# Turning merged branches, x2 and the MLP's inner layer: TensorE transposes replaced by 32x32 VectorE transposes and a pass through memory

## The chip, the cores and the metric

The kernel runs on one core of a Trainium2 chip. A core has a matrix engine (TensorE, "PE" in the profile, with its weight loads as "PEld"), a vector engine (VectorE, "DVE"), a scalar engine (ScalarE, "ACT"), GpSimd ("POOL") and SyncE ("SP"). Each runs its own instruction stream in order, and they wait for one another through semaphores. SP issues the DMAs of the weights, POOL most of the others; 16 DMA engines carry them out. SBUF is the on-chip memory of 128 partitions; PSUM holds what TensorE writes. The metric is the device time of one execution in microseconds, lower is better.

## What is computed

One layer of a decoder on 256 tokens of 2048 features, in float32. Three mixers read one input projection; their outputs are projected, gated, summed and projected again, and an MLP follows. Cut to what matters here:

```python
for l in range(DEPTH):                                   # DEPTH = 1
    u = rms_norm(x, attn_norm[l])
    proj = jnp.einsum('bsd,de->bse', u, w_in[l])
    ...
    o_fox = fox_mixer(...); o_mla = mla_mixer(...); o_gdn = gdn_mixer(...)      # each (1, 256, 1024)
    gates = jax.nn.sigmoid(gate.astype(jnp.float32)).reshape(B, S, N_BRANCHES, D_MODEL)
    merged = (gates[:, :, 0] * jnp.einsum('bsc,cd->bsd', o_fox, w_branch[l, 0])
              + gates[:, :, 1] * jnp.einsum('bsc,cd->bsd', o_mla, w_branch[l, 1])
              + gates[:, :, 2] * jnp.einsum('bsc,cd->bsd', o_gdn, w_branch[l, 2]))
    x = x + jnp.einsum('bsd,de->bse', merged, w_out[l])
    h = rms_norm(x, mlp_norm[l])
    h = jnp.square(jax.nn.relu(jnp.einsum('bsd,df->bsf', h, w_up[l])))          # (1, 256, 8192)
    x = x + jnp.einsum('bsf,fd->bsd', h, w_down[l])
return rms_norm(x, final_norm)
```

## The kernel before

**Products.** All large products run through `gemm` (L211). Weights stream from memory; the activations lie in SBUF, turned: features on the partitions, tokens along the free axis, because TensorE contracts over partitions. Activations and weights are both split into two exact parts, a high one (rounded to the type `F32R`) and the rest; three passes (high x high, high x low, low x high) are summed in PSUM. So each product needs its left side as `H` and `L`, tiles of [128 features, 16 feature tiles, 256 tokens] made by `hl_pair` (L155).

`gemm` takes a block of 512 output columns at a time, with two PSUM tiles (one for each half of the tokens, `t` = 0 and 1). A block has `KT / 2` steps (KT = 16 row tiles, 8 in the branches). In a step a weight chunk of 256 rows (`raw`, 4 buffers) is loaded by SP, ScalarE casts it to `wh` (L220), VectorE subtracts to get `wl` (L221; 3 buffers each), and TensorE runs 12 matmuls (L227 to L229). At the block's end the function `evac` is called for `t` = 0 and `t` = 1 and takes the result out of PSUM.

**Stages around the change.**
- Branches (L1002 to L1017): 4 column blocks `n`, each with 3 products `b` of KT = 8. `evac` multiplies with the sigmoid of the gates, which POOL loads from memory (L1007), and sums in `acc[t]`. After `b` = 2, `to_hl` (L990) turns `acc[t]` into the left side `mH`, `mL` of `w_out`.
- Output projection (L1026 to L1035): `out_evac` adds the product to the residual `x2` and sums squares (L1030); at `t` = 1, `transpose_pair` (L142, called at L1033) turns the 512 new columns of `x2`, multiplies with the gain of the norm and writes `hH`, `hL`.
- MLP (L1044 to L1062): 4 times, 4 blocks of `w_up`, whose `up_evac` takes relu, squares, and turns with `to_hl` into `dH`, `dL`; then 4 blocks (3 in the last round) of `w_down`.

So 512 columns that a block has produced become four row tiles of the next product. Those of the last block of a stage are needed in steps 6 and 7 of the next stage's first block.

`to_hl` does for one `t`: four TensorE transposes of 128x128 into a PSUM tile (L994), a ScalarE cast into `H` (L998) and a VectorE subtraction into `L` (L999). `transpose_pair` does the same for two column tiles and both `t`, with the gain (L147, L151, L152).

**Order.** The kernel is traced in the order of the Python code. When it is built (`schedule_with_timeline_sim=True`, L1122), a scheduler gives each engine a fixed order from a modelled timeline: among the instructions that the model holds ready, the one traced first. On the chip each engine then runs its order, whatever arrives late. Large tiles share 13 buffers of 8 KB per partition (tag "m8", made by `big`, L87); small work tiles of [128, 512] share 8 (tag "t2"). A tile whose tag has no free buffer waits until one is released.

Of the kernel before, what the change touches and what calls it, by code (L numbers as in the profile page):

```python
# [18 lines left out]
P = 128  # L19
# [14 lines left out]
WARM = 12  # L34

# [23 lines left out]
def decoder_kernel(ctx: ExitStack, tc: tile.TileContext, x, attn_norm, w_in, fox_fgate_bias, mla_q_norm,  # L59
# [73 lines left out]
    sel = cp.tile([P, 264], F32R, tag="sel", name="sel")  # 8 x [128, 32], column j of the j-th is 1  # L133
# [8 lines left out]
    def transpose_pair(src, ct0, kt0, g0, H, L):  # L142
        """Columns ct0, ct0 + 1 of src (128 each), both token tiles, times the gains g0, g0 + 1, into H/L(kt0), (kt0 + 1)."""
        pv = psx("tr").rearrange("p (a b) -> p a b", a=2)
        for a in range(2):
            for t in range(2):
                PE.transpose(pv[:, a, t * P:(t + 1) * P], src(t, ct0 + a), ident)  # L147
        for a in range(2):
            g = gcol[:, g0 + a:g0 + a + 1]
            hh = H(kt0 + a)  # L150
            A.activation(out=hh, in_=pv[:, a, :], func=AF.Copy, scale=g)  # L151
# [11 lines left out]
    def rsqrt_(dst, src, n, s):  # L163
        """dst = src ** -0.5 for [128, n] tiles of positive numbers."""
# [32 lines left out]
    def rstd_of(ss, parts, n, s, r=None):  # L197
        """(sum over the parts / n + eps) ** -0.5 per token tile -> [128, 2]."""
# [10 lines left out]
    CK = 2  # L209

    def gemm(lhsH, lhsL, W, row0, KT, blocks, evac):  # L211
        for bi, (c0, n) in enumerate(blocks):
            ps = [pm.tile([P, 512], F32, tag="mm", name=nm("mm")) for _ in range(2)]
            for kc in range(0, KT, CK):
# [7 lines left out]
                for kk in range(CK):  # L222
                    k = kc + kk
                    for t in range(2):
                        sl = slice(t * P, (t + 1) * P)
                        last = k == KT - 1
                        PE.matmul(ps[t][:, :n], lhsT=lhsH(k)[:, sl], rhs=wh[:, kk, :n], start=(k == 0), stop=False)  # L227
                        PE.matmul(ps[t][:, :n], lhsT=lhsH(k)[:, sl], rhs=wl[:, kk, :n], start=False, stop=False)  # L228
                        PE.matmul(ps[t][:, :n], lhsT=lhsL(k)[:, sl], rhs=wh[:, kk, :n], start=False, stop=last)  # L229
# [6 lines left out]
    def run(*gens):  # L236
        """Trace generators to their ends, one after another."""
# [4 lines left out]
    def weave(main, side):  # L242
        """Trace main with one step of side behind each of its steps."""
# [12 lines left out]
    def w_cols(blocks, evac):  # L256
        return gemm(uH, uL, w_in, 0, 16, blocks, evac)
# [44 lines left out]
    def softplus_parts(z, n, s):  # L302
        """log1p(exp(-|z|)) and exp(-|z|)."""
# [75 lines left out]
    lat = big("lat", tag="m8a").rearrange("p (t c) -> p t c", t=2)  # L379
    latk = sp.tile([P, 2, 72], F32, tag="latk", name="latk")  # forget logits, rotary key  # L380
# [30 lines left out]
    def load_split(src, n):  # L411
        """A weight of 512 rows, n columns at most 512, as [128, 4, n], in two exact parts: 2 x two row tiles."""
# [21 lines left out]
    def by_feature(w, H, L, dst, scale):  # L434
        """dst: [128, 4, 256] <- four heads of 128 features."""
# [22 lines left out]
    def rope(dst, src, t, nh):  # L458
        """dst, src: [128, nh, 64]."""
# [106 lines left out]
    def fox_decay():  # L566
# [5 lines left out]
        nl = small([P, 16], "nl")  # -log f  # L572
# [6 lines left out]
        ncum = small([P, 16], "ncum")  # -cumulative log f  # L579
# [14 lines left out]
    def fox():  # L594
# [72 lines left out]
    def gdn():  # L667
        V.tensor_tensor(out=zg.rearrange("p t (h d) -> p (t h) d", d=HD), in0=zg.rearrange("p t (h d) -> p (t h) d", d=HD),
                        in1=onorm.unsqueeze(1).broadcast_to([P, 16, HD]), op=ALU.mult)
        # z[:, 0] = a + dt_bias, z[:, 1] = b  # L670
# [20 lines left out]
        # cumulative log decay in each chunk of 128, and its total  # L691
# [23 lines left out]
        ex = small([P, 16], "ex")  # exp(g_total - g) of chunk 0, exp(g) of chunk 1  # L715
# [4 lines left out]
        # squared norms of k and q: columns (w, t, h)  # L720
# [32 lines left out]
        # Gram matrices  # L753
# [15 lines left out]
        # inverses of the 32 x 32 diagonal blocks by forward substitution, one block's half per partition  # L769
# [36 lines left out]
        # join them to 64 and to 128  # L806
        # (I + X')^-1 = D - D O D with O = X' between the blocks; of 128 columns, 64 change at a level
# [20 lines left out]
        def part(ap, lv, b):  # L828
            """Columns of [128, n, 128] in the even (b = 0) or odd blocks of 32 (lv = 0) or of 64 (lv = 1)."""
# [27 lines left out]
        # k of chunk 0 by tokens  # L857
# [7 lines left out]
        # outputs, chunk by chunk  # L865
# [3 lines left out]
        og = R  # a chunk's outputs take the place of its right-hand sides  # L869
# [45 lines left out]
        # scale, norm, gate  # L915
# [74 lines left out]
    def to_hl(src, H, L, n, t):  # L990
        """512 columns of a token tile, transposed, into H/L (lists of two [128, 8, 256])."""
        pt = psx("hl").rearrange("p (a t) -> p a t", a=4)
        for a in range(4):
            PE.transpose(pt[:, a, :], src[:, a * P:(a + 1) * P], ident)  # L994
        r = slice((n % 2) * 4, (n % 2) * 4 + 4)
        c = slice(t * P, (t + 1) * P)
        h = H[n // 2][:, r, c]
        A.copy(out=h, in_=pt)  # L998
        V.tensor_tensor(out=L[n // 2][:, r, c], in0=pt, in1=h.bitcast(F32), op=ALU.subtract)  # L999

    mH, mL, mHt, mLt = hl_pair("m")
    for n in range(4):  # L1002
        acc = [t2("acc") for _ in range(2)]
        for b in range(3):
            def evac(bi, t, ps, b=b, n=n, acc=acc):
# [8 lines left out]
                if b == 2:  # L1014
                    to_hl(acc[t], mHt, mLt, n, t)

            run(gemm(lambda k, b=b: oH[b][:, k, :], lambda k, b=b: oL[b][:, k, :], w_branch[0, b], 0, 8, [(n * 512, 512)], evac))  # L1017

# [7 lines left out]
    def out_evac(n, t, ps):  # L1026
# [8 lines left out]
    run(gemm(mH, mL, w_out[0], 0, 16, [(n * 512, 512) for n in range(4)], out_evac))  # L1035
# [8 lines left out]
    for c in range(4):  # L1044
        dH, dL, dHt, dLt = hl_pair("d")

        def up_evac(n, t, ps):
            r = t2("r")
            A.activation(out=r, in_=ps, func=AF.Relu)
            V.tensor_tensor(out=r, in0=r, in1=r, op=ALU.mult)  # L1050
            to_hl(r, dHt, dLt, n, t)

        run(gemm(hH, hL, w_up[0], 0, 16, [(c * 2048 + n * 512, 512) for n in range(4)], up_evac))
# [8 lines left out]
        run(gemm(dH, dL, w_down[0], c * 2048, 16, [(n * 512, 512) for n in range(4 if c < 3 else 3)], down_evac))  # L1062

# [62 lines left out]
```

## Time and profile before

| | us |
|---|---|
| timed runs, median of 3 (lowest, highest) | 1723.16 (1722.75, 1724.45) |
| span of the profiled execution, first to last instruction | 1721.6 |
| difference: median less span | 1.6 |

The page gives no time of its own for the profiled execution beside its span; what lies outside the span is put at the difference above. The granted TensorE clock is 0.997 of full speed over the span. The transposes in question show as groups of instructions:

```profile
L994 PE MATMUL hl<-cst,r x128: 270/272/273, 1027.9 to 1629.6; 128*128 128x128 f32 x128
L994 PE MATMUL hl<-cst,acc x32: 270/272/273, 814.7 to 916.1; 128*128 128x128 f32 x32
L147 PE MATMUL tr<-cst,xx x32: 270/273/273, 936.8 to 1005.8; 128*128 128x128 f32 x32
```

How to read it: a row of the answer for one tile has the line, the engine, the operation, what it writes and reads, how often, its shortest, median and longest duration in ns, and the first and last start in us. Matmuls are pipelined, and their ends are modelled, so durations of neighbours overlap; what one costs is seen in the distance between things that repeat. The chain of work that ended last follows the run backwards from its last instruction, at each step to what released it or to the instruction before it on its engine; only what lies on this chain can shorten the run directly. In a timeline row the bracket at the end gives the engine's idle time just before the instruction and what ended it.

### The profile page before, as it was taken

How to read it: one execution, taken by the hardware profiler on the slowest of the kernel's cores; microseconds unless marked ns; L12 is line 12 of the kernel's file. 1: busy time of each engine (PE TensorE's matmuls, PEld its weight loads, DVE VectorE, ACT ScalarE, POOL GpSimd, SP SyncE). 2: the span in 40 equal slices, each digit the busy share in tenths (PEclk: the TensorE clock that was granted, in tenths of full speed). 3: DMA queues.
4: the chain of work that ended last, by engine and by line, in shares of the span. 5: the costliest groups of instructions: out<-in, count | busy, mean ns of one | idle time of the engine just before them, and what ended most of it. 6: DMA issues, size and time to landing. Idle time of an engine off the chain costs nothing.

```text
span 1721.6 us, 21456 instructions
## 1 busy us (share of the span) xinstructions
PE 1705.6 (99%) x8131; PEld 1433.8 (83%) x8131; DVE 1018.7 (59%) x1388; ACT 799.7 (46%) x1019; POOL 51.6 (3%) x91
## 2 busy tenths in 40 slices
PE   8999999999999999999999999999999999999997
PEld 8997889978788898888888888888888888888886
DVE  5755455676668946646665565555555555555555
ACT  5554446555534434544544544434443344334443
POOL 1000000000010100001100000000000000000000
PEclk9999999999999999999999999999999999999999
DMA  7755464766667745767776566556655665566553
GB/s 214 211 163 181 142 177 133 223 202 179 174 177 217 220 122 158 257 218 262 243 276 201 183 184 192 186 193 190 189 186 194 190 188 186 192 193 187 185 193 140
DMA packets 183209, 331.49 MB, mean 193 GB/s; under 512 B 15577, under 2 KB 42401, under 8 KB 181953
## 3 DMA queue, kind: packets, MB, share of 16 engines
q1 hardware_dynamic: 176816, 307.54, 58.4%
q0 software_dynamic: 5968, 22.05, 3.8%
q8 instruction: 64, 1.05, 0.3%
q10 hardware_dynamic: 320, 0.53, 0.1%
q14 instruction: 41, 0.33, 0.1%
HBM read 319.05 MB, written 11.03 MB: 192 GB/s over the span
## 4 chain that ended last, share of the span: by engine, by line
PE 76%; DVE 1%; DMA 1%; issue 1%; ACT 0%; DVEq 0%; SPq 0%; ACTq 0%; POOLq 0%
PE mm L228 24%; PE mm L229 24%; PE mm L227 24%; PE hl L994 1%; DMA of<-of_d 0%; PE mm L1088 0%; PE mm L1087 0%; PE mm L1086 0%; PE pO L843 0%; PE pD L851 0%; DMA E<-gcd 0%; PE pg L762 0%; PE cv L633 0%; DVE wl L221 0%; PE oo L909 0%
## 5 line engine op out<-in xcount | busy, mean ns | idle before, releaser
L221 DVE TENSOR_TENSOR wl<-raw,wh 128x1024 fp32r<-128x1024 f32 (+4 forms) x568 | 678.8, 1196 | 557.3 <-ACT wh L220 552.2
L220 ACT CAST wh<-raw 128x1024 fp32r<-128x1024 f32 (+4 forms) x568 | 585.4, 1031 | 721.3 <-PE mm L229 680.1
L228 PE MATMUL mm<-wl,uH 128*128 128x512 f32 (+4 forms) x960 | 367.1, 383 | 1.7 <-DVE wl L221 1.6
L229 PE MATMUL mm<-wh,uL 128*128 128x512 f32 (+4 forms) x960 | 363.2, 379 | 0.0
L227 PE MATMUL mm<-wh,uH 128*128 128x512 f32 (+4 forms) x960 | 336.9, 382 | 0.0
L228 PEld LDWEIGHTS mm<-wl,uH 128*128 128x128 f32 x960 | 180.9, 188 | 32.9 <-DVE wl L221 3.1
L229 PEld LDWEIGHTS mm<-wh,uL 128*128 128x128 f32 x960 | 180.9, 189 | 29.5
L227 PEld LDWEIGHTS mm<-wh,uH 128*128 128x128 f32 x960 | 179.8, 189 | 30.8 <-issue 1.0
L229 PE MATMUL mm<-wh,hL 128*128 128x512 f32 x512 | 200.2, 391 | 0.0
L228 PE MATMUL mm<-wl,hH 128*128 128x512 f32 x512 | 199.4, 389 | 0.0
L229 PE MATMUL mm<-wh,dL 128*128 128x512 f32 x480 | 187.1, 390 | 0.0
L228 PE MATMUL mm<-wl,dH 128*128 128x512 f32 x480 | 186.8, 389 | 0.0
L227 PE MATMUL mm<-wh,hH 128*128 128x512 f32 x512 | 182.8, 389 | 0.0
L227 PE MATMUL mm<-wh,dH 128*128 128x512 f32 x480 | 168.6, 389 | 0.0
L228 PEld LDWEIGHTS mm<-wl,hH 128*128 128x128 f32 x512 | 96.1, 188 | 20.0
L227 PEld LDWEIGHTS mm<-wh,hH 128*128 128x128 f32 x512 | 96.1, 188 | 19.5
L229 PEld LDWEIGHTS mm<-wh,hL 128*128 128x128 f32 x512 | 96.1, 188 | 19.5
L228 PEld LDWEIGHTS mm<-wl,dH 128*128 128x128 f32 x480 | 90.1, 188 | 18.8
L227 PEld LDWEIGHTS mm<-wh,dH 128*128 128x128 f32 x480 | 90.1, 188 | 18.6
L229 PEld LDWEIGHTS mm<-wh,dL 128*128 128x128 f32 x480 | 90.1, 188 | 18.4
L228 PE MATMUL mm<-wl,mH 128*128 128x512 f32 x128 | 50.1, 392 | 0.0
L229 PE MATMUL mm<-wh,mL 128*128 128x512 f32 x128 | 49.8, 389 | 0.0
(412 smaller groups left out, 1585.1 us busy)
## 6 DMA issues: line engine op xcount, KB each, us to landing
raw<-in_w_in_dram SPq DMA_DIRECT2D x192, 512.0 KB, 3.9
raw<-in_w_up_dram SPq DMA_DIRECT2D x128, 512.0 KB, 3.7
raw<-in_w_down_dram SPq DMA_DIRECT2D x128, 512.0 KB, 4.5
raw<-in_w_branch_dram SPq DMA_DIRECT2D x48, 512.0 KB, 4.8
raw<-in_w_out_dram SPq DMA_DIRECT2D x32, 512.0 KB, 3.8
gd<-ge POOLq DMA_DIRECT2D x24, 256.0 KB, 3.9
gate<-gd POOLq DMA_DIRECT2D x24, 256.0 KB, 4.7
raw<-in_w_in_dram SPq DMA_DIRECT2D x16, 368.0 KB, 3.9
```

The lines of the kernel that those rows point to most:

```text
L220: A.copy(out=wh[:, :, :n], in_=raw[:, :, :n])
L221: V.tensor_tensor(out=wl[:, :, :n], in0=raw[:, :, :n], in1=wh[:, :, :n].bitcast(F32), op=ALU.subtract)
L227: PE.matmul(ps[t][:, :n], lhsT=lhsH(k)[:, sl], rhs=wh[:, kk, :n], start=(k == 0), stop=False)
L228: PE.matmul(ps[t][:, :n], lhsT=lhsH(k)[:, sl], rhs=wl[:, kk, :n], start=False, stop=False)
L229: PE.matmul(ps[t][:, :n], lhsT=lhsL(k)[:, sl], rhs=wh[:, kk, :n], start=False, stop=last)
L994: PE.transpose(pt[:, a, :], src[:, a * P:(a + 1) * P], ident)
```

## The change

The transposes of the merged branches, of `x2` and of the MLP's inner layer leave TensorE. Per block of 512 columns, `turned` takes both token halves: two VectorE transposes, which turn each 32x32 square in place of its own, write a tile `z`; one DMA from POOL's queue writes `z` to a buffer in DRAM, and four more (one for each group of 32 partitions) read it back into `y` so that the squares land on their partitions. `z` and `y` are the halves of one "m8" tile. The casts and subtractions that make `H` and `L` out of `y` (`halves_of`) are not traced at once but through `later`: `gemm` calls `tick` after each step, and after TURN = 4 steps the function is run. For `x2` the gain is applied to `y` by four ScalarE instructions ahead of that (`gained`). `by_tile` only passes the token half on; the matmuls stay the same. `transpose_pair` remains for the start of the kernel. The diff, without the comments that it drops:

```diff
+TURN = 4
...
+    pending = []
+    def later(steps, f):
+        pending.append([steps, f])
+    def tick():
+        for p in pending:
+            p[0] -= 1
+        while pending and pending[0][0] <= 0:
+            pending.pop(0)[1]()
+    def by_tile(f):
+        return lambda k, t: f(k)[:, t * P:(t + 1) * P]
...
                     for t in range(2):
-                        sl = slice(t * P, (t + 1) * P)
                         last = k == KT - 1
-                        PE.matmul(ps[t][:, :n], lhsT=lhsH(k)[:, sl], rhs=wh[:, kk, :n], start=(k == 0), stop=False)
...
+                        PE.matmul(ps[t][:, :n], lhsT=lhsH(k, t), rhs=wh[:, kk, :n], start=(k == 0), stop=False)
...
+                tick()
                 if kc + CK < KT:
                     yield
...
-    def to_hl(src, H, L, n, t):
-        pt = psx("hl").rearrange("p (a t) -> p a t", a=4)
-        for a in range(4):
-            PE.transpose(pt[:, a, :], src[:, a * P:(a + 1) * P], ident)
+    def turned(src, then):
+        zy = big("zy")
+        z, y = zy[:, 0:1024], zy[:, 1024:2048]
+        zv = z.rearrange("p (j t k b) -> p t k j b", j=4, t=2, k=4)
+        for t in range(2):
+            V.transpose(out=zv[:, t], in_=src[t].rearrange("p (k j b) -> p k j b", k=4, j=4))
+        d = dp.tile([P, 1024], F32, tag="turn", name=nm("turn"), bufs=4)
+        nc.gpsimd.dma_start(out=d, in_=z)
+        dv = d.rearrange("(g a) (j x) -> j a g x", a=32, j=4)
+        for j in range(4):
+            nc.gpsimd.dma_start(out=y[32 * j:32 * j + 32].rearrange("a (g x) -> a g x", g=4), in_=dv[j])
+        later(TURN, lambda: then(y))
+
+    def halves_of(y, n, H, L):
         r = slice((n % 2) * 4, (n % 2) * 4 + 4)
-        c = slice(t * P, (t + 1) * P)
-        h = H[n // 2][:, r, c]
-        A.copy(out=h, in_=pt)
-        V.tensor_tensor(out=L[n // 2][:, r, c], in0=pt, in1=h.bitcast(F32), op=ALU.subtract)
+        yv = y.rearrange("p (g t k b) -> p t k g b", g=4, t=2, k=4)
+        for t in range(2):
+            h, l = (z[n // 2][:, r, t * P:(t + 1) * P].rearrange("p k (g b) -> p k g b", b=32) for z in (H, L))
+            A.copy(out=h, in_=yv[:, t])
+            V.tensor_tensor(out=l, in0=yv[:, t], in1=h.bitcast(F32), op=ALU.subtract)
...
-                if b == 2:
-                    to_hl(acc[t], mHt, mLt, n, t)
+                if b == 2 and t == 1:
+                    turned(acc, lambda y: halves_of(y, n, mHt, mLt))
...
         if t == 1:
-            for a in range(0, 4, 2):
-                transpose_pair(lambda tt, k: x2[tt][:, k * P:(k + 1) * P], n * 4 + a, n * 4 + a, 16 + n * 4 + a, hH, hL)
+            turned([x2[tt][:, n * 512:(n + 1) * 512] for tt in range(2)], lambda y: gained(y, n))
+
+    def gained(y, n):
+        yv = y.rearrange("p (gt k b) -> p k gt b", gt=8, k=4)
+        for k in range(4):
+            A.activation(out=yv[:, k], in_=yv[:, k], func=AF.Copy, scale=gcol[:, 16 + 4 * n + k:17 + 4 * n + k])
+        halves_of(y, n, hHt, hLt)
...
         dH, dL, dHt, dLt = hl_pair("d")
+        rr = {}
 
         def up_evac(n, t, ps):
-            r = t2("r")
+            r = rr[t] = t2("r")
             A.activation(out=r, in_=ps, func=AF.Relu)
             V.tensor_tensor(out=r, in0=r, in1=r, op=ALU.mult)
-            to_hl(r, dHt, dLt, n, t)
+            if t == 1:
+                turned([rr[0], rr[1]], lambda y: halves_of(y, n, dHt, dLt))
```

More of the change, by code (lines that the diff above doesn't have):

```diff
@@ L256, in w_cols @@
     def w_cols(blocks, evac):
-        return gemm(uH, uL, w_in, 0, 16, blocks, evac)
+        return gemm(by_tile(uH), by_tile(uL), w_in, 0, 16, blocks, evac)
     def split_blocks(c0, c1):
@@ L1060, in down_evac @@
                 A.activation(out=j, in_=xb, func=AF.Square, accum_out=ss3[:, t, n:n + 1])
-        run(gemm(dH, dL, w_down[0], c * 2048, 16, [(n * 512, 512) for n in range(4 if c < 3 else 3)], down_evac))
+        run(gemm(by_tile(dH), by_tile(dL), w_down[0], c * 2048, 16, [(n * 512, 512) for n in range(4 if c < 3 else 3)], down_evac))
     m3 = small([P, 2], "m3")
```

11 lines of the change are left out of this document (6 added, 5 removed).

## The prediction

> **What bounds the kernel now.** I read the page's busy row and chain first, then the chain piece by piece around the stages that the diff touches, then the timeline of one block end, then the DMA rows.
>
> ```profile
> PE 1705.6 (99%) x8131; PEld 1433.8 (83%) x8131; DVE 1018.7 (59%) x1388; ACT 799.7 (46%) x1019; POOL 51.6 (3%) x91
> PE 76%; DVE 1%; DMA 1%; issue 1%; ACT 0%; DVEq 0%; SPq 0%; ACTq 0%; POOLq 0%
> 1096.06 0.87 PE hl L994 x8
> 1205.75 0.87 PE hl L994 x8
> 1228.40 0.87 PE hl L994 x8
> 814.81 0.87 PE hl L994 x8
> 848.35 0.87 PE hl L994 x8
> 937.44 0.66 PE tr L147 x6
> 960.10 0.66 PE tr L147 x6
> ```
>
> TensorE is busy 99% of the span and the chain that ended last runs over it. The last seven rows are pieces of that chain (start, length): the transposes to be removed are on it, with no gap of TensorE around them. Their price is read from spacings, not from durations, since matmuls overlap. Two neighbouring blocks of `w_up` stand 1228.40 - 1205.75 = 22.65 us apart: one block and one set of eight transposes. From 1096.06 to 1205.75 lie five blocks (four of `w_down`, one of `w_up`) and one set, 109.69 us. So four blocks are 87.04 us, a block 21.76 us (a step, an eighth of it, 2.72), and a set 0.9 us. `w_out` repeats this (22.66). The branches agree: 33.54 us for three blocks of half the rows (32.64) and a set.
>
> **What is removed.** Sets: 4 in the branches, 4 in `w_out`, 16 in `w_up`; 24 x 0.9 = 21.6 us of TensorE, all on the chain. Nothing else leaves it. The PSUM tiles of these transposes go too; nobody waits for one there.
>
> **What is added.** Per set: two VectorE transposes of 128x512, one 512 KB write and four 128 KB reads from POOL's queue, and two ScalarE casts and two VectorE subtractions that now read `y` in SBUF instead of PSUM. `w_out` has four more ScalarE gains. Here is the end of a `w_up` block, with the steady steps behind it:
>
> ```profile
> 1223.03 0.61 PE L227 MATMUL mm<-wh,hH 128*128 128x512 f32 x2
> 1222.54 1.28 ACT L1049 ACTIVATE r<-mm 128x512 f32<-128x512 f32 x2 [0.98 <-PE mm L229]
> 1223.17 1.38 DVE L1050 TENSOR_TENSOR r<-r 128x512 f32<-128x512 f32 x2 [0.36 <-ACT r L1049]
> 1235.00 1.05 ACT L220 CAST wh<-raw 128x1024 fp32r<-128x1024 f32 x1 [1.67 <-PE mm L229]
> 1236.09 1.22 DVE L221 TENSOR_TENSOR wl<-raw,wh 128x1024 fp32r<-128x1024 f32 x1 [1.49 <-ACT wh L220]
> 1234.96 0.45 PE mm L227 x2
> 1240.40 0.45 PE mm L227 x2
> L998 ACT CAST dH<-hl x32: 586/589/593, 1028.6 to 1630.0; 128x512 fp32r<-128x512 f32 x32
> L999 DVE TENSOR_TENSOR dL<-hl,dH x32: 678/686/693, 1029.2 to 1630.7; 128x512 fp32r<-128x512 f32 x32
> L151 ACT ACTIVATE hH<-tr,gcol x16: 465/467/475, 937.8 to 1008.0; 128x256 fp32r<-128x256 f32 x16
> ```
>
> Call the block's end T0 (1223.03 here). `r` is finished at 1224.55, T0 + 1.5. In a steady step ScalarE and VectorE each idle about 1.5 us of 2.72. The cast at 1235.00 starts as TensorE frees a buffer (1234.96), and with three buffers TensorE needs it two steps later, at 1240.40: `wh` is ready 4.35 us early, `wl` (1237.31) 3.1 us early. This lead is what hides the new work.
>
> *VectorE transposes.* The trace has none. The nearest rows are the 128x512 subtraction (0.69) and the 128x1024 one (1.22). I take 0.69, for the size; two end at T0 + 2.9 (T0 + 4.0 at the upper bound). VectorE's idle time covers them; in front of `wl` they use 1.4 us of its 3.1.
>
> [...]
>
> *The passage through memory.*
>
> ```profile
> gd<-ge POOLq DMA_DIRECT2D x24, 256.0 KB, 3.9
> of_d<-of POOLq DMA_DIRECT2D x1, 1024.0 KB, 5.2
> DMA to landing us min/median/max: 2.3/3.9/7.1
> 777.89 2.66 POOL L1007 DMA_DIRECT2D gate<-gd  x5
> DMA to landing us min/median/max: 3.6/4.7/9.4
> DT<-td POOLq DMA_DIRECT2D x8, 32.0 KB, 5.7
> 593.07 0.59 POOL L803 DMA_DIRECT2D DT<-td  x1 [1.11 <-DMA td<-NT]
> 593.92 3.89 POOL L803 DMA_DIRECT2D DT<-td  x7 [0.27 <-issue]
> ```
>
> These are writes and reads from POOL's queue, with issue rows; the two landing rows belong to `gd<-ge` and to `gate<-gd`. The write (512 KB, between 256 KB at 3.9 and 1024 KB at 5.2) I take at 4.5, bounds 2.3 to 7.1. POOL waits for it, then issues four reads 0.53 us apart (2.66 / 5), the last 1.6 us after the first; landing I take at 4.7 from `gate<-gd`, bounds 3.6 to 9.4. So `y` is there at Y = T0 + 2.9 + 4.5 + 1.6 + 4.7 = T0 + 13.7; bounds T0 + 10.4 and T0 + 22. In `w_out` the adds finish about 0.5 us sooner, in the branches some 0.7 later.
>
> *Who waits for `y`.* First, the **handover**: the last block's features are row tiles 12 to 15 of the next product, needed in its step 6 at T0 + 6 x 2.72 = T0 + 16.3. With the first cast at Y + 0.6 = 14.3 and its subtraction at 15.0, there is room. This happens six times (branches to `w_out`, `w_out` to `w_up`, four times `w_up` to `w_down`). After `w_out` four gains come first, about 4 x 0.47 = 1.9 us, and the low half is ready at 16.4: on the edge, worth some tenths.
>
> Second, and at all 24: **the queues of ScalarE and VectorE run in order.** The scheduler places the casts by its own modelled time; if `y` lands later on the chip, every `wh` behind them waits. Behind `wh` of step 5 (T0 + 8.2 to 9.2) they would hold up `wh` of step 6: it would end at Y + 2.25, `wl` at Y + 3.5, and TensorE needs that `wl` at T0 + 16.5. The loss is Y - 13.0, here 0.7. Behind `wh` of step 6 (which starts at T0 + 10.9) the limit is one step later, 15.7: nothing. Before has three such waits:
>
> ```profile
> 703.45 1.91 ACT L983 CAST ofH<-of 128x2048 fp32r<-128x2048 f32 x1 [3.13 <-DMA of<-of_d]
> 709.87 1.92 ACT L983 CAST omH<-om 128x2048 fp32r<-128x2048 f32 x1 [1.38 <-DMA om<-om_d]
> 366.29 3.23 DVE L712 TENSOR_SCALAR E<-E,gc 128x128 f32<-128x128 f32 x16 [2.17 <-DMA E<-gcd]
> 708.88 0.50 PE L228 MATMUL mm<-wl,uH 128*128 128x512 f32 x1 [0.58 <-DVE wl L221]
> ```
>
> An engine stood 1.4 to 3.1 us before a load that was placed too early, and TensorE lost only 0.58 us behind the longest. If the new passages are misjudged alike, the model has `y` at T0 + 10.6 to 12.3 and puts the casts mostly behind `wh` of step 6. I take no loss there, and 3 us in all for the edges of both kinds (an eighth of a microsecond each).
>
> *Other costs taken at nothing.* POOL: it is busy 3%, and its other work here is gate loads and two early loads, for which no compute engine waits in the trace; if the passages pushed gate loads back until one did, ScalarE's sigmoid would wait in front of a `wh`, as the casts do. Weights: the passages add 1 MB per block,
>
> ```profile
> raw<-in_w_up_dram SPq DMA_DIRECT2D x128, 512.0 KB, 3.7
> 1112.00:1133.70 21.70, 21.70 (x97) 17.99 (x96) 11.06 (x11) 8.45 (x8) 0.00 (x0) 1.00 0.60 194
> POOL fg L1042 <- PE mm L229: 15.3, 1, 15.3
> ```
>
> to a stage whose DMA engines are 60% busy at 194 GB/s (the last two figures of the window row; the figure before is the granted clock): 48 GB/s more. A weight buffer freed with `wl` at 1237.31 is needed four steps after 1235.00, at 1245.88: 8.6 us against 3.7 to land. Buffers: `zy` takes one of the 13 of tag "m8". `w_up` holds 11 (h 4, d 4, x2 2, fg 1) and a passage lives under a block, so two are enough; in `w_out` the count is tightest, and the last row shows what a shortage looks like (POOL waiting for a buffer). There it cost nothing; a VectorE transpose that waited so would hold up `wl`.
>
> **The sum.** The span was 1721.6 us; the median of the timed runs is 1723.2, so 1.6 us lie outside and stay. 1723.2 - 21.6 + 3 = 1704.6 us. The floor, with nothing lost, is 1701.6.
>
> **The rivals.**
>
> *Partly given back* (0.11): passages land near their limits, Y about 14, and half of the casts stand one step too early, so that 0.4 to 0.75 us per set return: 1712 to 1720 us. For it: Y by medians is within a microsecond of 13.0. *No change* (0.08): 0.75 to 1.05 us return per set, 1720 to 1727.
>
> *Slower* (0.17): ScalarE's queue. The casts stand ahead of `wh` of step 6 and `y` lands after T0 + 13.9: from there the loss, Y - 13.0, exceeds the 0.9 that a set saves. At Y = 15, 24 x 2.0 = 48 us return: 1749.6. For it: the spread of `gate<-gd` up to 9.4, two transfers in a row, and the too early placements above. Against it: those cost TensorE little, a later arrival in the model moves the casts one step back, and the four reads are only 512 KB together.
>
> *The reads follow one another* (0.02). Eight loads `DT<-td`, issued within 4.7 us, each landed in about 5.7: they overlapped. If the four did not, they would need 4 x 3.6 = 14.4 us from the first issue, Y would be T0 + 21.8, and behind `wh` of step 6 the loss 21.8 - 15.7 = 6.1 us per set: 1848. [...] The eight rows speak against it for transfers this small.
>
> *It doesn't shorten TensorE's work* (in the 0.08): the transposes would have to lie in gaps; the spacing of 22.65 against 21.76 speaks against that.
>
> **How the numbers follow.** The forecast, 1700 to 1712, has 0.62. Faster by over 0.2% (below 1719.7): 0.62 + 0.11 = 0.73; within 0.2%, about what a measurement of this kernel can tell from no change: 0.08; slower: 0.17 + 0.02 = 0.19. The range 1700 to 1728 takes in the forecast, the two middle cases and the mildest of the slower ones.
>
> **What would show it.** Right: blocks of `w_up` and `w_out` 21.76 us apart, no idle of TensorE, casts of `y` starting about T0 + 14 with ScalarE idle under 3 us before them. Wrong: ScalarE idle before the cast, put down to the reads of `y`, and TensorE waiting for `wl` in step 6; or TensorE waiting for `mL`, `hL` or `dL` at the six handovers; or a VectorE transpose well over 1.2 us.

## The result, and the profile after

| | before | after |
|---|---|---|
| timed runs beside each other, median (lowest, highest), us | 1723.18 (1722.75, 1724.45) | 1735.9 (1734.43, 1738.82) |
| ratio after / before, 95% interval | | 1.0071 (1.0058 to 1.0083) |
| span of the profiled execution, us | 1721.6 | 1735.3 |
| granted clock | 0.997 | 0.994 |

The kernel became slower by 12.7 us, where 1704.6 us was predicted. (Two executions on record, one of e4 below and one of the kernel before, ran at a granted clock of 0.75 and 0.72 from start to end and count in no ratio.) The 24 sets of transposes did leave TensorE, and more than their time came back. The page of the changed kernel (busy row, chain, issues with the median time to landing):

```profile
PE 1696.7 (98%) x7939; PEld 1413.5 (81%) x7939; DVE 1040.9 (60%) x1428; ACT 801.8 (46%) x1027; POOL 117.5 (7%) x211
PE 30%; DMA 5%; issue 2%; ACT 1%; DVE 1%; POOL 1%; DVEq 0%; ACTq 0%; POOLq 0%
raw<-in_w_up_dram SPq DMA_DIRECT2D x128, 512.0 KB, 4.5
raw<-in_w_out_dram SPq DMA_DIRECT2D x32, 512.0 KB, 5.7
turn<-zy POOLq DMA_DIRECT2D x24, 512.0 KB, 3.4
zy<-turn POOLq DMA_DIRECT2D x96, 128.0 KB, 6.1
```

TensorE's 192 transposes are gone (8131 - 7939 instructions), but it is busy only 8.9 us less, not 21.6; three spells of half clock (last section) would account for some 5 us of the difference, and the rest stays open. DMA has 5% of the chain, 1% before. The reads take 6.1 us each to land, and the loads of `w_up` 4.5 instead of 3.7. Who stands for the passages is read from the view of the waits (engine and line, waited for; us in total, times, longest):

```profile
ACT dH L1030 <- DMA zy<-turn: 68.6, 16, 5.5
ACT zy L1071 <- DMA zy<-turn: 17.7, 3, 7.8
ACT mH L1030 <- DMA zy<-turn: 15.7, 4, 4.4
DVE dL L1031 <- ACT dH L1030: 58.9, 16, 4.9
PE mm L243 <- ACT wh L237: 8.8, 5, 3.4
PE mm L244 <- DVE wl L238: 8.4, 15, 1.8
PE mm L243 <- ACT dH L1030: 4.4, 4, 1.2
```

ScalarE stands 102 us in 23 of the 24 passages, in front of the casts (or gains) that read `y`; what stands behind it is then late for TensorE: `wh`, `wl`, and four times `dH` at a handover. One set of the MLP, the last block of the first round, in the timeline (start, length, engine, line; in brackets the idle time before and its releaser):

```profile
1106.58 0.61 PE L243 MATMUL mm<-wh,dH 128*128 128x512 f32 x2
1108.02 1.30 DVE L1016 STREAM_TRANSPOSE zy<-r 128x512 f32<-128x512 f32 x2
1109.62 0.56 POOL L1018 DMA_DIRECT2D turn<-zy  x1 [15.82 <-DVE zy L1016]
1113.49 2.19 POOL L1021 DMA_DIRECT2D zy<-turn  x4 [3.32 <-ACT wh L237]
1117.66 1.05 ACT L237 CAST wh<-raw 128x1024 fp32r<-128x1024 f32 x1 [1.67 <-PE mm L245]
1123.44 1.14 ACT L1030 CAST dH<-zy 128x512 fp32r<-128x512 f32 x2 [4.72 <-DMA zy<-turn]
1124.11 0.50 PE L243 MATMUL mm<-wh,dH 128*128 128x512 f32 x1 [1.04 <-ACT dH L1030]
```

T0 is 1106.58. `z` is finished at T0 + 2.7 (2.9 predicted), the reads are issued 3.87 us after the write (4.5 predicted), the casts stand behind `wh` of step 6 (as predicted), and `y` comes at T0 + 16.9 (13.7 predicted): 9.95 us after the first read was issued, not 1.6 + 4.7 = 6.3. TensorE, at its handover, waits 1.04 us. Before the MLP it is worse; the first set of `w_out`, with a row of the windows view of TensorE's time around it (the third figure from the end is the granted clock):

```profile
950.65 1.05 ACT L237 CAST wh<-raw 128x1024 fp32r<-128x1024 f32 x1 [1.66 <-PE mm L245]
959.51 1.70 ACT L1071 ACTIVATE zy<-zy,gcol 128x256 f32<-128x256 f32 x4 [7.82 <-DMA zy<-turn]
962.20 0.73 PE L243 MATMUL mm<-wh,mH 128*128 128x512 f32 x2 [3.43 <-ACT wh L237]
960.00:968.00 8.00, 5.27 (x15) 3.90 (x16) 5.82 (x8) 6.70 (x14) 0.00 (x0) 0.79 0.32 105
```

ScalarE stands 7.82 us, TensorE 3.43 us, and after that the clock is at half for 3.4 us.

**Where the time went.** One and the same matmul, counted in TensorE's own order without the transposes, can be looked up in both traces. The lag of the changed kernel is +2.1 us at the first matmul of the branches, up to which both kernels have run the same instructions (the load of `E` landed later, and one spell of half clock followed), +1.6 at the first of `w_out`, +15.4 at the end of the first block of `w_up` (called the entry below), and +13.3 after the last set. So the sets of the branches and of `w_out` lose 13 us, nearly all of it from the branches' handover on, and the 16 of the MLP win 2.1 us of the 14.4 that were to be won there. The evictions (`acc`, `xx`, `r`) mislead at this place: by the second one of `w_up` the lag would be 18.0 us and the win of the MLP 4.8, and the expectation for e8 goes by that. But 109 matmuls of the stage had started at the second eviction, against 97 in the kernel before: TensorE's order has a step of the next block ahead of the block's last matmuls.

### The profile page after: what moved, and what is told of

It is laid out like the page before. It is cut to its first block, busy times and chain, and to the rows that moved or that the text cites. A ratio compares the mean times of both kernels' runs of the same rounds, so it can differ in the third digit from the quotient of the medians.

```text
span 1735.3 us, 21340 instructions
## 1 busy us (share of the span) xinstructions
PE 1696.7 (98%) x7939; PEld 1413.5 (81%) x7939; DVE 1040.9 (60%) x1428; ACT 801.8 (46%) x1027; POOL 117.5 (7%) x211
## 3 DMA queue, kind: packets, MB, share of 16 engines
q0 software_dynamic: 14032, 47.22, 9.2%
## 5 line engine op out<-in xcount | busy, mean ns | idle before, releaser
L243 PE MATMUL mm<-wh,hH 128*128 128x512 f32 x512 | 179.3, 391 | 1.7 <-ACT wh L237 1.7
L1018 POOL DMA_DIRECT2D turn<-zy x24 | 13.4, 557 | 677.0 <-DVE zy L1016 658.5
L1021 POOL DMA_DIRECT2D zy<-turn x96 | 52.5, 553 | 96.0 <-issue 27.8
```

Of the source, the lines that this page charges most:

```text
L243: PE.matmul(ps[t][:, :n], lhsT=lhsH(k, t), rhs=wh[:, kk, :n], start=(k == 0), stop=False)
L1018: nc.gpsimd.dma_start(out=d, in_=z)
L1021: nc.gpsimd.dma_start(out=y[32 * j:32 * j + 32].rearrange("a (g x) -> a g x", g=4), in_=dv[j])
```

## The experiments

Each time was taken beside runs of the kernel before (1722.6 to 1724.4 us by their medians); ratios are to those, with 95% intervals. Edits are against the changed kernel.

### Without the passage: e1_no_passage

```diff
-        d = dp.tile([P, 1024], F32, tag="turn", ...)
-        nc.gpsimd.dma_start(out=d, in_=z)
...
-        later(TURN, lambda: then(y))
+        later(TURN, lambda: then(z))
```

> Leaves out the passage through memory: the casts read the VectorE transposes' own tile z, so the squares stay on the wrong partitions. Theory A (the loss is ScalarE standing in its queue before a y that lands after T0 + 15.7, with everything behind it): all 24 sets of TensorE transposes are saved, 1701 to 1706 us. Rival B (the passages' traffic holds up the weights): the same here, 1701 to 1706. Rival C (the added work itself costs it: VectorE transposes of 0.70 us in front of wl, casts and subtractions from SBUF in runs of 32): little changes, 1725 to 1736.

1703.11 us (0.9881, 0.9866 to 0.9896), span 1701.6. The floor of the prediction, with nothing lost, was 1701.6: 1.5 us beside it. VectorE's transposes, the casts from SBUF and the four gains cost TensorE next to nothing; the loss is in the passage.

### The passage, but nobody waits for y: e2_not_waited

```diff
-        later(TURN, lambda: then(y))
+        later(TURN, lambda: then(z))
```

> All DMAs of the passage are issued as in the changed kernel, but the casts read z and nobody waits for y (in w_out the gains, which write into z, still wait for the write to DRAM). Theory A: the wait is gone, 1701 to 1708 us. Rival B (traffic): still 1728 to 1736, with ScalarE waiting for weights. Rival C: 1725 to 1736.

1706.33 us (0.9905, 0.9890 to 0.9921). All the traffic together costs 3.2 us over e1; the remaining 29.6 us of the changed kernel are the wait for `y` and what it brings with it (no spell of half clock falls inside this kernel's trace). The waits and issues of this kernel:

```profile
ACT dH L1030 <- DVE zy L1016: 7.1, 16, 0.5
zy<-turn POOLq DMA_DIRECT2D x96, 128.0 KB, 5.9
raw<-in_w_up_dram SPq DMA_DIRECT2D x128, 512.0 KB, 3.9
```

The reads take as long here (5.9 against 6.1) with no engine standing: they are not slow because of the jam.

### One read in place of four: e3_one_read

```diff
-        for j in range(4):
-            nc.gpsimd.dma_start(out=y[32 * j:32 * j + 32].rearrange("a (g x) -> a g x", g=4), in_=dv[j])
+        nc.gpsimd.dma_start(out=y, in_=d)
```

> The four reads of 32 partitions in runs of 1 KB become one read of 128 partitions in rows of 4 KB; the same bytes, but the squares stay on the wrong partitions. The casts wait for y as before. Theory A with the reads as the term that was mis-sized: y lands 3 to 4 us earlier (about 5 us from issue instead of 8 to 9.9 from the first issue), before T0 + 15.7 in the MLP, and most sets are saved: 1706 to 1716 us. If the shape of the reads doesn't matter and only the bytes on a busy queue do: y as late as now, 1728 to 1736.

1715.53 us (0.9958, 0.9944 to 0.9972). The same 512 KB in one read of all 128 partitions give 20 us back, though the casts stand one step further forward here, behind `wh` of step 5. The same set as above, from its timeline:

```profile
1098.97 0.53 POOL L1019 DMA_DIRECT2D zy<-turn  x1 [3.18 <-ACT wh L237]
1104.49 1.14 ACT L1028 CAST dH<-zy 128x512 fp32r<-128x512 f32 x2 [2.85 <-DMA zy<-turn]
```

From issue to cast 5.5 us instead of 9.95.

### Casts further back: e4_late_casts and e12_late_again

```diff
-            pending.pop(0)[1]()
+            f = pending.pop(0)[1]
+            with tc.issue_after(cast[0]):          # the wh cast issued last
+                f()
...
-        later(TURN, lambda: then(y))
+        later(8 if n < 3 else 6, lambda: then(y))
```

> Same work and DMAs, but the casts of the first three blocks of each stage are queued behind the wh of the eighth step instead of the seventh; those of the last block, which the next stage needs in its seventh step, stay. Theory A: the 18 first sets lose little (limit T0 + 18.4 instead of 15.7), the six handovers lose 1 to 3 us each, more after the branches and w_out: 1708 to 1718 us. Rival B (traffic) or C (added work): 1728 to 1736, since neither goes away.

1730.52 us (1.0042, 1.0026 to 1.0059): a miss. e12 is the same kernel, with a trace to read:

> The kernel of e4_late_casts once more, for a profile at an undisturbed clock. Theory of the handovers: MLP blocks 0 to 2 win 0.9 us each without a wait of ScalarE, the last blocks lose 1 to 2 us each, and w_out and the entry to the MLP lose 12 to 18 us as in the changed kernel; 1725 to 1733 us. Against it: waits for y of over 2 us in blocks 0 to 2 of the MLP.

1732.26 us (1.0041, 1.0028 to 1.0054). Its waits:

```profile
ACT dH L1034 <- DMA zy<-turn: 38.2, 16, 5.4
ACT zy L1075 <- DMA zy<-turn: 19.5, 4, 8.7
ACT mH L1034 <- DMA zy<-turn: 11.3, 4, 3.4
```

In the MLP it does what it should: blocks 0 to 2 win 0.9 us each in all rounds but for one block of the first, and the lag falls from +18.3 at the entry to +9.9. The last blocks lose at most 1.3 us net (-0.2, -0.8, +0.4, +1.3), mostly less than the 1 to 2 expected. What spoils it lies ahead: +18.3 us at the entry, more than the +15.4 of the changed kernel. Expecting e4 to win had put too much of the loss into the MLP.

### Only by the narrowness, or by the number of reads: e5_four_wide

```diff
-            nc.gpsimd.dma_start(out=y[32 * j:32 * j + 32].rearrange("a (g x) -> a g x", g=4), in_=dv[j])
+            nc.gpsimd.dma_start(out=y[:, j * 256:(j + 1) * 256], in_=d[:, j * 256:(j + 1) * 256])
```

> The four reads stay four, of 128 KB each and in pieces of 1 KB, but each fills all 128 partitions of 1 KB of y instead of 32 partitions of 4 KB (the values of y then stand in the order in which they left, so the products are made of wrongly placed values; the work is the same). Theory A, the 32 partitions: transfers into a quarter of the partitions hold one another and the weights up, four wide ones do not; 1711 to 1719 us, as with the single read (1715.5), reads landed about 6.5 us after their first issue. Theory B, the number of reads or the length of their pieces: no change against the changed kernel, 1731 to 1739 us, reads landed 9 to 10 us after their first issue.

1716.22 us (0.995, 0.9935 to 0.9965), in the range of theory A. Read `j` fetches the very same bytes from memory as in the changed kernel; only where they go differs. Its waits:

```profile
ACT dH L1029 <- DMA zy<-turn: 28.5, 16, 2.7
ACT mH L1029 <- DMA zy<-turn: 9.5, 4, 3.2
ACT zy L1070 <- DMA zy<-turn: 14.4, 4, 7.9
```

Neither the 96 reads nor their pieces of 1 KB make the changed kernel lose; their number alone costs something, 7.0 us from the first issue to the cast against 5.4 in e3. In the MLP every set is won (the lag falls from +6.0 to -8.3, 14.3 us of 14.4); what remains is lost ahead of the entry.

### The narrow transfers moved to the writing side: e6_four_writes

```diff
-        nc.gpsimd.dma_start(out=d, in_=z)
+        for g in range(4):
+            nc.gpsimd.dma_start(out=dv[g], in_=z[32 * g:32 * g + 32].rearrange("a (j x) -> a j x", j=4))
...
+        nc.gpsimd.dma_start(out=y, in_=d)
```

> The blocks are rearranged on the way out: four writes of 32 partitions each, then one read of all 128 partitions in rows of 4 KB. Theory A1, transfers on 32 partitions of on-chip memory are slow in either direction: the four writes land about 9 us after their first issue, the read 5 us later, so y stands at T0 + 17 or later and the time is 1730 to 1745 us. Theory A2, only those that write into 32 partitions are slow: the writes land about 5.5 us after their first issue, y stands at T0 + 14, and the time is 1708 to 1719 us.

1736.98 us (1.0076, 1.0056 to 1.0097): A1. The read goes out 7.4 us after the first write, where it was 3.9:

```profile
1107.14 2.18 POOL L1020 DMA_DIRECT2D turn<-zy  x4 [14.46 <-DVE zy L1016]
1114.50 0.56 POOL L1021 DMA_DIRECT2D zy<-turn  x1 [5.17 <-DMA turn<-zy]
```

What the read gains, the writes lose.

### Which stages lose: e7_last_by_pe_late and e8_mlp_only

In e7 the last block of each stage (`n == 3`) is turned by TensorE as in the kernel before, and the casts of the others stand as in e4; in e8 branches and `w_out` keep TensorE, and the MLP is as changed.

```diff
-            elif t == 1:
-                turned([rr[0], rr[1]], lambda y: ...)
+            if n == 3:
+                to_hl(r, dHt, dLt, n, t)
+            elif t == 1:
+                turned([rr[0], rr[1]], n, lambda y: ...)
```

> Casts of the blocks n = 0 to 2 behind the wh cast of step 7, and the last block of each stage turned by TensorE as in the kernel before: 18 sets are left. If the handovers at the last blocks are what kept the late casts at 1730.5 us, nothing waits for y any more: 18 x 0.9 = 16.2 us less work, 3 us for the traffic, 1707 to 1713 us. If the late casts lose in the first three blocks (y later than the cast behind step 7, or weights held up by the reads), the time stays at 1718 to 1729 us.

1714.02 us (0.9939, 0.9924 to 0.9954), 1 us above its range; the twelve MLP sets win 10.7 us and the six others nothing (a lag of +0.7 at the first matmul of the branches and at the entry).

> Branches and x2 turned by TensorE as in the kernel before, only the MLP's inner layer by the passage. By the place of the evictions the changed kernel loses about 18 us between the branches' end and the first w_up block and wins 4.8 us in the MLP: 1716 to 1720 us if these losses belong to their stages. If the ScalarE queue loses in the MLP what it seemed to lose before it, 1724 to 1736 us.

1722.43 us (0.9991, 0.9981 to 1.0), 2.4 us above its range; lag -0.6 at the entry, -3.9 at the end of the MLP. So the losses do belong to their stages: without the sets of branches and `w_out` nothing is lost there, and the MLP wins 3.3 us.

### Reads of all partitions with the right result: e9, e10, e11

```diff
-        dv = d.rearrange("(g a) (j x) -> j a g x", a=32, j=4)
+        dv = d.rearrange("(g a) (j x) -> g j a x", a=32, j=4)
...
-            nc.gpsimd.dma_start(out=y[32 * j:32 * j + 32]..., in_=dv[j])
+            nc.gpsimd.dma_start(out=y[:, g * 256:(g + 1) * 256], in_=dv[g])
```

> The whole change, with the four reads cut the other way: read g fetches, for all 128 partitions of y, the 1 KB that came from the 32 partitions of group g of z; the result is the same. If it is the quarter of the partitions that held y up, this is as e5_four_wide: 1711 to 1719 us, reads landed about 6.5 us after their first issue, MLP sets of 0.9 us each won. If the order in which off-chip memory is read matters (here each read takes rows from all over the buffer's columns), reads land 8 us or more after their first issue: 1722 to 1737 us.

> The reads of e9_wide_reads, in the MLP alone; branches and x2 by TensorE as before. In e5_four_wide the first set after the entry and all later ones of the MLP are won whole and only the stages before it lose: 16 x 0.9 = 14.4 us off, about 1 us for the traffic, 1707 to 1711 us. If the losses of branches and w_out come back at the entry to the MLP, whose first sets are then the first to wait, 1712 to 1719 us.

> As e10_wide_mlp, and the first three sets of the branches turned by VectorE too; the last, which hands over to w_out, stays with TensorE. If the branches lose only at their handover, 3 x 0.9 = 2.7 us less than e10_wide_mlp: 1704 to 1709 us. If the gates' loads in that stage hold the passage up, as much as e10_wide_mlp or 1 to 3 us more: 1707 to 1714 us.

All three missed: 1763.51 us (1.023, 1.0211 to 1.025), 1742.19 (1.0099, 1.0073 to 1.0124) and 1741.23 (1.0115, 1.0085 to 1.0145). These reads fill all 128 partitions and are slower than the narrow ones: 9.8 us to the cast. Their queue, first in the changed kernel and then in e9 (packets, MB, share of the engines):

```profile
q0 software_dynamic: 14032, 47.22, 9.2%
```

```profile
q0 software_dynamic: 23248, 47.37, 9.2%
```

The 9216 packets more are of 16 bytes, three to each packet of 4 KB. So all partitions are not enough; how a transfer is cut matters too. Whether it is the small packets or the order of the pieces that costs the time, these runs do not tell apart.

### The scale of the range, and the cut: e13 to e16

e13 keeps the quarters but reads whole rows, e16 reads two halves; e14 and e15 rearrange on the way out.

```diff
+            nc.gpsimd.dma_start(out=y[32 * j:32 * j + 32], in_=d[32 * j:32 * j + 32])                      # e13, 4 times
+            nc.gpsimd.dma_start(out=y[64 * j:64 * j + 64], in_=d[64 * j:64 * j + 64])                      # e16, twice
+        nc.gpsimd.dma_start(out=d.rearrange("(j p) x -> p j x", j=4), in_=z.rearrange("p (j x) -> p j x", j=4))   # e14; reads d[(j g a), x], outermost j
+            nc.gpsimd.dma_start(out=dv[j], in_=z[:, j * 256:(j + 1) * 256])                                # e15, dv[j] is [g a x]; one read
```

> Four reads into 32 partitions each, as in the changed kernel, but each fetches whole rows of 4 KB that lie one behind another (the values then stay in their quarter, so the products are made of wrongly placed values). Theory E, engines that meet in a quarter of the partitions: packets stay at 0.25 us or more, reads land 9 to 10 us after their first issue, 1729 to 1740 us. Theory S, scattered pieces: packets of 0.16 to 0.19 us, reads land about 6.3 us after their first issue, 1709 to 1719 us.

1728.23 us (1.003, 1.0016 to 1.0044): between the two ranges, but the packets of 0.28 us and the 8.9 us to the cast go with theory E's figures (0.25 or more, 9 to 10); that engines meet in a quarter was the author's estimate of the cause, and no run shows it. That the pieces lie apart adds some 0.4 us (9.3 in the changed kernel).

> z is written as four blocks [j] of 128 rows of 1 KB by one DMA, and read g takes for each of four groups of 32 neighbouring partitions of y 32 KB that lie together; the result is the same. Theory E: the write takes 3.9 us as before; the reads are fast only if the pieces of a packet go to neighbouring partitions, then as in e5_four_wide about 6.5 us and 1711 to 1719 us, else 9 us and 1745 to 1765 us as in e9_wide_reads. Theory S: the reads are fast, but the write, whose pieces of a packet go 128 KB apart, takes 6 us or more, 1722 to 1738 us.

1775.45 us (1.0301, 1.0286 to 1.0316): above every range; the write takes 4.8 us and the reads 9.5.

> Four writes, each of 1 KB of all 128 partitions of z to its quarter of the rows of y, and one read of all 128 partitions in rows of 4 KB; the result is the same. Theory E: the writes land about 6 us after their first issue, the read 5.1 us after its own, y at T0 + 15: 1716 to 1727 us, if the pieces of a packet come from neighbouring partitions. Theory S: the writes take 8 to 9 us as with four writes of 32 partitions (e6_four_writes): 1732 to 1742 us.

1835.19 us (1.0643, 1.0625 to 1.0661), far above both ranges: the four writes need 11.2 us until the read can go out.

> Two reads into 64 partitions each, in whole rows of 4 KB (values then stay in their half, so the products are made of wrongly placed values). If the price follows the range, it lies between whole and quarter: cast 6.5 to 7.7 us after the first issue (5.4 with one read, 8.9 with four), y near T0 + 14, 1714 to 1722 us. If only a transfer below all 128 partitions matters, not how far below, as the quarters: 8.3 us or more, 1724 to 1732 us. If only the number of reads matters, one issue more than the single read: 6.0 us and 1713 to 1717 us.

1747.8 us (1.0141, 1.0125 to 1.0156). The cast comes 7.0 us after the first read, as by the range; the time misses by 26 us. Its timeline shows why:

```profile
1099.18 1.03 POOL L1020 DMA_DIRECT2D zy<-turn  x2 [3.19 <-issue]
1100.75 1.05 ACT L237 CAST wh<-raw 128x1024 fp32r<-128x1024 f32 x1 [1.67 <-PE mm L245]
1106.96 1.14 ACT L1029 CAST dH<-zy 128x512 fp32r<-128x512 f32 x2 [5.15 <-DMA zy<-turn]
```

Here the casts stand behind `wh` of step 5: the scheduler, which goes by its own model of the time, moved them one step forward when two reads took the place of four (and with the single read of e3). There the limit is T0 + 13.0 and not 15.7, and `y` came at 14.1. e18 moves the casts back and leaves the reads alone (the edit of e4 on e16):

> Two reads into 64 partitions each as in e16_half_rows, and the casts of blocks 0 to 2 behind the wh cast of step 7; the last blocks' casts keep their place behind wh of step 5. If the place of the casts is what cost e16_half_rows its 24 us, MLP blocks 0 to 2 win 0.9 us each and the whole is 1716 to 1732 us. If the reads themselves (or the weights they hold up) cost it, the time stays at 1738 to 1750 us.

1718.15 us (0.9971, 0.9962 to 0.9981): 30 us from the place of a cast in a queue. In front of the MLP's casts ScalarE stands 79.6 us in e16, in all 16 sets, and 27.3 us in e18, in nine.

The medians of the 16 MLP sets of each kernel, from the records of instructions and single packets in its trace: us from the first read's issue to its last packet's end and to the cast, mean length of a 4 KB packet of the reads and of a 2 KB packet of the weights meanwhile, `y` after T0, the step behind whose `wh` the casts stand (that of most sets; in e18 the casts of blocks 0 to 2 mostly wait for their place, not for `y`). Then TensorE's lag to the kernel before at the entry and after the last set, and its change between the two. The last column works that change out from the prediction's own account: the time by which each set's `y` comes after the limit for its casts (T0 + 13.0 behind `wh` of step 5, T0 + 15.7 behind step 6, 2.72 more for each step further back), added up over the 16 sets, less 16 x 0.9, plus half the length of the spells of half clock in the MLP.

```
                   packets  cast  4 KB    2 KB    y     step   lag in    out   change  worked out
e3_one_read           5.0    5.4  0.202   0.093   12.2    5       1.2  -10.1    -11.2     -10.9
e5_four_wide          6.3    7.0  0.181   0.096   13.7    6       6.0   -8.3    -14.3     -14.4
e16_half_rows         6.1    7.0  0.271   0.111   14.1    5      14.3   24.4     10.1      12.9
e18_half_late         5.7    7.9  0.267   0.110      -   7, 5     5.4   -7.4    -12.8     -12.2
e13_quarter_rows      7.8    8.9  0.276   0.117   15.8    6       9.9    6.3     -3.6      -1.6
the change            8.2    9.3  0.287   0.119   16.5    6      15.4   13.3     -2.1      -2.3
e9_wide_reads         8.2    9.8  0.270   0.127   17.1    6      27.0   40.9     14.0      15.4
e14_block_write       8.3    9.5  0.290   0.120   17.7    6      28.7   53.6     24.9      26.6
e15_column_writes     5.0    5.4  0.167   0.100   19.8    6      40.8  115.9     75.1      84.2
```

Two things are to be seen. The change of the lag follows the last column, within 3 us but for e15: in the MLP a late `y` costs what it comes after the limit of its casts, and with the casts behind step 6 the balance turns between `y` at 16.5 and 17.1, as it should (the limit of 15.7 and the 0.9 us that a set saves are 16.6). And packets of the reads are short, and those of the weights beside them too, only where a transfer goes to all partitions without rearranging: 0.167 to 0.202 and 0.093 to 0.100 us in e3, e5 and e15, 0.267 to 0.290 and 0.110 to 0.127 in the others.

### The best version: e17_mlp_late

The MLP's blocks 0 to 2 alone, with the casts behind step 7 and the reads of the changed kernel (the edits of e7 and e8).

> The changed kernel's own reads, in the MLP's blocks n = 0 to 2 alone, casts behind the wh cast of step 7; branches, x2 and the last blocks by TensorE as before: 12 sets of 0.9 us = 10.8 us off. If the late casts fail only at the handovers and before the MLP, nothing waits for y: 1711 to 1714 us. If y is later than the place behind step 7 at times, or the reads hold the weights up, 1715 to 1722 us.

1712.15 us (0.9935, 0.9918 to 0.9951), in range, and faster than both kernels. TensorE's waits in it are those of the kernel's start and two short ones:

```profile
PE tr L148 <- DMA x<-in_x_dram: 4.1, 2, 3.8
PE mm L248 <- DVE wl L242: 1.1, 2, 0.6
PE warm L126 <- DVE ones L110: 1.1, 1, 1.1
```

The twelve sets win 10.7 us (lag from -0.7 to -11.4), 0.9 each: where nobody waits for the passage, the change gives what the spacings promised.

## Why the prediction was wrong

- **The 0.9 us per set** was right, and so was the floor (1701.6 against 1703.1 in e1).
- **VectorE's transposes.** Taken at 0.69:

```profile
L1016 DVE STREAM_TRANSPOSE zy<-r x32: 668/703/712, 1040.2 to 1638.5; 128x512 f32<-128x512 f32 x32
```

  0.70 us, as the 128x512 subtraction (0.69) and well under the 128x1024 one (1.22).
- **The write**, at 4.5 until the first read, took 3.87 by the median of the MLP, and 5.1 to 7.3 in the branches and the first two sets of `w_out`.
- **The landing of the reads is the step that failed.** It was 6.3 us from the first issue (1.6 + 4.7, the 4.7 from `gate<-gd`); it was 9.3 by the median of the MLP, and T0 + 13.7 became T0 + 16.5. `gate<-gd` and `DT<-td` were the wrong rows to measure it by. One read of all partitions takes 5.4 us to the cast (e3) and four take 7.0 (e5), about what three further issues of 0.53 add; two into halves take 7.0 (e16), 1.1 more than one read and one further issue; four into quarters in plain rows take 8.9 (e13), 1.9 more than four of all partitions, and their cut into pieces of 1 KB makes it 9.3.
- **What does tell e5 from the change** is how long a packet takes: 4 KB packets take 0.276 us into quarters (e13) and 0.271 into halves (e16), against 0.18 to 0.20 into all 128 partitions (e5, e3). Why a packet takes longer there, these runs do not show; nor do the packets tell why halves end sooner than quarters (6.1 us to the last packet against 7.8). e9, e14 and e15 reach all partitions and are slow all the same: 9.8 and 9.5 us to the cast, and 11.2 us from the first write until the read can go out. In e15 the writes' first 4 KB packets start in groups of four (1.28, 1.32, 1.34, 1.43 us after the issue; then 1.80, 1.80, 1.84, 2.00), while in e6, with four writes too, 16 start between 1.13 and 1.35. But the reads of e9, which run among the weights' packets, show no such groups, and 16-byte packets come with every one of these transfers (23248 packets in the queue of each of the three kernels, 14032 in the changed kernel's). What makes them slow is therefore not shown: which engine moved a packet, no view here tells, and no version with the right result and plain transfers of all partitions both ways was found.
- **Where the casts stand** was right for the MLP (behind `wh` of step 6 in 15 of 16 sets; in the branches and `w_out` mostly one step further back), and so were both limits: 15.7 there (e13 at 15.8 still wins, e9 at 17.1 loses) and 13.0 one step earlier (e16 at 14.1 wins nothing). That the scheduler moves them when the number of reads changes had been counted against the slower rival; in e16 it did the harm.
- **The handovers**, given room at T0 + 16.3, were late by the same term: four waits for `dH` of at most 1.2 us in the MLP, whose last blocks lose 0.5 to 0.6 us each where the others win up to 0.9.
- **3 us for the edges** became 33 (1735.9 against 1703.1 in e1). By the prediction's own limit, `y` at 16.5 gives back 0.8 us per set, 24 x 0.8 = 19 us, which would have been about 1724 with its 3 us; the late read alone, at the MLP's median, is "no change" and not a loss. Two thirds of the 33 lie ahead of the entry (a lag of +15.4 against -5.7 in e1): there the eight sets of branches and `w_out` lose 13 us where 7 were to be won. In the last set of the branches and the first three of `w_out` `y` came at T0 + 20.2 to 22.6, with a longer write; gains of 1.7 us stand in front of the next `wh`, and spells of half clock came on top. e3 loses far less there (2.4 us), so the reads' form is most of it; what share each of the others has was not told apart.
- **The traffic**, taken at nothing, costs 3.2 us (e2).
- **The rivals.** "Slower" had the mechanism (ScalarE's queue, a `y` too late) but another condition: not casts one step too early but reads 3 us too late for the right step. "The reads follow one another" had a later `y`, but at T0 + 21.8 where 16.5 came, and so too large a price for it; it was put aside at 0.02 on rows of a transfer that fills other partitions in another form.

## What to carry to other kernels

Here the form of its transfers set the price of a pass through memory before their bytes did: the same 512 KB took 5.4 us to the cast in one plain read of all partitions and 9.3 in four of 32, and the packets of the weights beside it were longer (0.119 us against 0.093). A load whose result an in-order engine reads needs its arrival compared with the place of that reader in the queue; moving the reader back two steps was worth 30 us here (e16, e18), and it must be looked up anew after each edit, because the scheduler moves it by its own model. Turn only the blocks that have slack: twelve of 24 sets, with their casts moved back, made the kernel 0.65% faster; all 24 made it 0.7% slower, and 0.4% slower with the casts moved back (e12).

## What was not expected of the hardware

Short stands of TensorE brought more than their length. After idling 3.43 us at 962.20, matmuls that had started 0.23 us apart started 0.43 apart:

```profile
957.70 0.39 PE L245 MATMUL mm<-wh,mL 128*128 128x512 f32 x1
957.93 0.39 PE L243 MATMUL mm<-wh,mH 128*128 128x512 f32 x1
...
964.81 0.63 PE L245 MATMUL mm<-wh,mL 128*128 128x512 f32 x1
965.24 0.63 PE L243 MATMUL mm<-wh,mH 128*128 128x512 f32 x1
```

The clock records of the traced executions have three such spells of 3.4 us at half speed inside the changed kernel (none inside the kernel before, e3 or e17), some 1.7 us of work each; the first came after an idle of only 1.78 us. e15 has 20 of 3.4 or 6.8 us. Within a trace all spells begin on one raster of 3.413 us; in the changed kernel, at 373.1, 963.6 and 1011.4 us, they stand 590.5 and 47.8 us apart, 173 and 14 times that. Over the traces of this document (all but e4's; the first 50 and the last 15 us of each left out) the raster's stretch just ahead of each of the 61 spells holds 1.63 us or more of idle time of TensorE (1.78, 2.54 and 2.03 in the changed kernel), and of the 9086 stretches that no spell followed none holds more than 1.83: in these traces about half a stretch of idle time, in one piece or in two, was followed by half clock in the next.

And the narrow reads touch their neighbours, if by less than their own packets: 2 KB packets of the weights' loads in the MLP, 0.102 us by the mean of all while no read runs (0.104 in the kernel before), take 0.119 beside the changed kernel's reads and 0.093 beside the single read of e3, by the medians of the table above.
